# First modulation quarter loaded in halves ahead of the weights, its row ahead of the broadcast, and products on zeros on TensorE

## The chip, the cores and the metric

The kernel runs on one core of a Trainium2 chip. The metric is the device time of one execution in microseconds; lower is better. Before the change it is 1782.46 us, the median of three runs (1781.53 to 1785.64). The profile comes from one more execution, which took 1778.15 us.

## The reference

The computation is one inference step of a small hybrid model: 128 context tokens and 512 latent tokens of width 1024 pass through two layers. The first layer is a Mamba-2 mixer, the second is differential attention; each is followed by a gated convolutional channel mixer. The change touches only what comes first: the conditioned norm ahead of the Mamba-2 mixer, and the first products with its input weights.

```python
def modulation(cvec, w, b):
    m = jax.nn.silu(cvec) @ w + b
    return jnp.split(m[:, None, :], 6, axis=-1)

def modulate(x, g, shift, scale):
    return rmsnorm(x, g) * (1 + scale) + shift
# layer 0
hp = modulate(xp, norm_mix_g[i], p_sh1, p_sc1)   # context tokens, conditioned by c_ctx
hs = modulate(xs, norm_mix_g[i], s_sh1, s_sc1)   # latent tokens, conditioned by c
proj = h @ in_w                                  # inside ssd_mixer
```

So before the first product with `in_w`, three things must exist: the root mean square of every token, the shift and scale of each channel (a product of SiLU(c) with 1024 x 2048 numbers of the modulation weights), and the scaled tokens.

## The kernel before

The tokens stand transposed: eight tiles `x0` to `x7` of 128 channels by 640 tokens (512 latent, 128 context). The function `first_tiles` holds everything that the change touches. It runs under a hand-written order: each engine executes its instructions in the order in which the code emits them, and waits only where data is missing. Nearly every instruction goes through helpers, so the profile gives one line (L95) for all of them; the tile names tell them apart.

- **Loads.** One queue, SP's, issues all loads of this stage in order: the condition `c`, the constants `cst`, the eight `x` tiles, two weight tiles `raw` (first the narrow one for dt, then the first full one), two small tables (`modb`, `gains`), the first quarter of the modulation weights (`mp`, eight transfers of 256 KB), a third weight tile, and the three other quarters. One transfer waits for the eighth before it.
- **The silu of the condition** (`s`) is made ahead of all this, by ScalarE and two VectorE instructions, from `c`.
- **Statistics.** ScalarE and VectorE square the `x` tiles in turn (`sq`); TensorE sums them with a matrix of ones into `ms`. VectorE makes the reciprocal root from it in nine small instructions (`rs_v`, `rs_a`, `rs_y`), and TensorE spreads the result over 128 partitions (`nbc`).
- **Modulation.** `rows(q, k0, k1)` multiplies `s` with a quarter of the modulation weights into four row strips (`modrow`). ScalarE copies them (`modrow_s`); `finish(q)` transposes them on TensorE (`modt`), adds the bias (`mod`) and makes the gain (`gs`) on VectorE. A quarter q holds shift and scale for the tiles 2q and 2q+1.
- **Operands.** `cast(u)` splits a weight tile into a rounded part `whi` (ScalarE) and the rest `wlo` (VectorE). `scaled(i)` multiplies `x` with the spread root (`h`, VectorE). `high(i)` makes the rounded, modulated operand `h00h` on ScalarE and the same number unrounded on VectorE (`h`, a TENSOR_SCALAR); `low(i)` subtracts them into `h00l`.
- **Products.** `dense(tiles, k)` adds, for channel tile k and each weight tile, three products into PSUM: `h00h` with `whi` (operation 0), `h00h` with `wlo` (1) and `h00l` with `whi` (2). The `rows` of the next quarter stand between them.

After this stage the Mamba-2 mixer runs under a scheduler that sets the order on each engine from its own reckoning; from the channel mixer on, the order is the same in both kernels.

Of the kernel before, what the change touches and what calls it, by code (L numbers as in the profile page):

```python
# [355 lines left out]
class Step:  # L356
# [220 lines left out]

    def rms_bcast(self, alloc, sq, t0, t1, count, wait=4, behind=False):


        n = (t1 - t0) // 4
        y = self.rms_rows(sq, t0, n, count, behind)
# [6 lines left out]
    def rms_rows(self, sq, t0, n, count, behind=False):  # L589

        ms = self.bank("m", "ms")
        gate = self.last if behind else None
        for i, s in enumerate(sq):
            for j in range(4):
                o = self.mm(ms[32 * j:32 * j + 32, :n], self.ones, s[:, t0 + j * n:t0 + (j + 1) * n],
                            i == 0, i == len(sq) - 1)
                if behind:
                    self.hold(o, [gate])
        y = self.pc.tile([P, 160], F32, tag="rs_y", name="rs_y", bufs=1)[:, :n]
        with self.urgent(1.6) if self.later else nullcontext():  # L600
            self.rsqrt(y, ms[:, :n], n, count)
        return y
# [221 lines left out]
    def first_tiles(self, h, pool):  # L824
# [12 lines left out]

        def rows(q, k0, k1):

            if k0 == 0:  # L840
                self.rowps = self.bank("y", "modrow")
            for k in range(k0, k1):
                for j in range(4):
                    self.mm(self.rowps[32 * j:32 * j + 32, :P], self.s32[:, k, :], parts[q][:, k, j * P:(j + 1) * P],
                            k == 0, k == KT - 1)
            if k1 == KT:
                self.row = self.slot("f", "modrow_s", bufs=NF)
                self.act(self.row[:, :P], self.rowps[:, :P], AF.Copy)

        def finish(q):  # L850
            pt = self.bank("m", "modt")
            nc.tensor.transpose(pt[:, :P], self.row[:, :P], self.ident)
            i0 = 2 * q
            mv = self.mod[0][:, 0:16, :].rearrange("p (s i) c -> p s i c", s=2)[:, :, i0:i0 + 2, :]
            bv = self.modb[:, 0:16].rearrange("p (s i) -> p s i", s=2)[:, :, i0:i0 + 2]
            self.tt(mv, pt[:, :P].rearrange("p (s i r) -> p s i r", s=2, i=2)[:, :, :, 0:2],
                    bv.unsqueeze(3).to_broadcast([P, 2, 2, 2]), ALU.add)
            self.stt(gs[:, i0:i0 + 2, :], self.mod[0][:, 8 + i0:10 + i0, :], 1.0,
                     self.gains[:, i0:i0 + 2].unsqueeze(2).to_broadcast([P, 2, 2]), ALU.add, ALU.mult)

# [5 lines left out]
        def high(i):  # L866
# [5 lines left out]
            for a0, b0, c in cond:  # L872
                nc.vector.tensor_scalar(f[:, a0:b0], t0[i][:, a0:b0], gs[:, i, c:c + 1], sh[:, i, c:c + 1], ALU.mult, ALU.add)

# [3 lines left out]

        def dense(tiles, k):

            for op in (0, 1, 2) if k < KT - 1 else (0, 2, 1):
                for ps, (hi, lo), m in tiles:
# [6 lines left out]
                    for p in "AB":  # L889
                        c0, c1 = HALF[p]  # L890
                        self.mm(ps[:n, PO + c0:PO + c1], wt, x[:, c0:c1], k + op == 0, k == KT - 1 and op == 1)

        self.cst = self.ct([P, 3 * P + 36], "cst")
        nc.sync.dma_start(self.cst, a["cst"])
        for i in range(KT):
            xi = self.xslot(f"x{i}")
            nc.sync.dma_start(xi, a["xT"][i])
            self.x.append(xi)
        self.prefetch(1)
        self.load_consts()  # L900
        gs, sh = self.gs[0][0], self.shift(0, 0)
        load(0)
        self.prefetch(2)
# [4 lines left out]
        for i in range(KT):  # L908
            if i % 2:
                self.tt(sq[i], self.x[i], self.x[i], ALU.mult)  # L910
            else:
                self.act(sq[i], self.x[i], AF.Square)
        st = self.rms_bcast(lambda: self.wide("nbc"), sq, 0, T, D)
        next(st)
        self.cast(0)
        self.cast(1)
        rows(0, 0, 3)
        try:
            next(st)
# [24 lines left out]
        for q in range(1, 4):  # L944
            k = 2 * q
            if q == 1:
                dense(ws[2:], 0)
                finish(q)
                dense(ws[2:], 1)
            else:  # L950
                dense(ws[:1], k - 1)
                finish(q)
                dense(ws[1:], k - 1)
# [1054 lines left out]
def _layout(i):  # L2008
# [8 lines left out]
    m = n["mod_w"][0]  # L2017
    d["modp"] = m[:, :2048].reshape(KT, P, 2, 4, 256).transpose(3, 1, 0, 2, 4).reshape(4, P, KT, 512)
    d["mod0"] = m[:, 2048:].reshape(KT, P, 4 * D)
# [58 lines left out]
```

## Time and profile before

| what | value |
|---|---|
| median of three runs | 1782.46 us (1781.53 to 1785.64) |
| the profiled execution | 1778.15 us, span 1776.4 us |
| mean granted TensorE clock | 0.997 |
| TensorE busy | 1741.9 us, 98% of the span |
| VectorE busy | 1471.9 us, 83% |
| ScalarE busy | 1169.3 us, 66% |
| first product with `in_w` | starts at 22.70 us |
| read from memory | 248.32 MB, 159 GB/s over the span |

The span runs from the first instruction to the last; the execution's own time is 1.75 us longer. A row of a timeline gives start, duration, engine, the operation with what it writes and reads, a count, and in brackets the idle time before it with what ended it. A row with a count above 1 lasts from the start of the first to the end of the last. [...]

### The profile page before, as it was taken

What the parts mean: (1) busy time and instruction counts of PE and PEld (TensorE: products, weight loads), DVE (VectorE), ACT (ScalarE), POOL (GpSimd) and SP (SyncE); (2) the same over time, 40 slices, a digit from 0 to 9 for tenths busy, and PEclk for the clock granted to TensorE, in tenths of its full rate; (3) what the DMA queues carried; (4) which work ended last, traced back from release to release, by engine and by line L of the source; (5) the groups of instructions that cost most, each with busy time, mean ns of one, the idle gap of its engine ahead of it and who ended that gap; (6) DMA issues with size and microseconds to landing.
All of it is one profiled execution on the core that took longest, in us unless ns stands there. A gap on an engine that the chain in (4) does not pass through costs nothing.

```text
span 1776.4 us, 33599 instructions
## 1 busy us (share of the span) xinstructions
PE 1741.9 (98%) x12786; PEld 1665.6 (94%) x12786; DVE 1471.9 (83%) x2947; ACT 1169.3 (66%) x2313; POOL 150.2 (8%) x180
## 2 busy tenths in 40 slices
PE   7999999999999999999999999999999999999997
PEld 5899898989989999999999999999889999999997
DVE  6689999999966879798689799899778677967686
ACT  3479696979624767666675578877547566756661
POOL 0000000000000111211210000000001012121210
PEclk9999999999999999999999999999999999999998
DMA  9844244445663686978877365666137458786882
GB/s 346 271 143 139 101 123 147 111 141 167 221 216 135 143 208 151 252 180 218 190 167 245 117 170 135 158 156 164 56 121 205 117 144 199 176 194 158 171 234 80
DMA packets 120206, 300.66 MB, mean 169 GB/s; under 512 B 13950, under 2 KB 21738, under 8 KB 120044
## 3 DMA queue, kind: packets, MB, share of 16 engines
q1 hardware_dynamic: 94636, 231.79, 40.5%
q0 software_dynamic: 24832, 66.20, 21.1%
q8 instruction: 100, 1.64, 0.4%
q14 instruction: 62, 0.51, 0.1%
q10 hardware_dynamic: 576, 0.52, 0.1%
HBM read 248.32 MB, written 34.80 MB: 159 GB/s over the span
## 4 chain that ended last, share of the span: by engine, by line
PE 74%; DVE 4%; ACT 1%; issue 1%; DMA 0%; DVEq 0%; ACTq 0%
PE up L95 28%; PE po L95 24%; PE st L95 4%; PE v L348 2%; PE q L348 2%; PE k L348 2%; PE z L95 2%; PE sl L348 2%; PE ov L348 1%; PE po L348 1%; PE wt L348 1%; PE yp L95 1%; PE nbc L95 1%; PE modrow L95 0%; DMA ml<-cv 0%
## 5 line engine op out<-in xcount | busy, mean ns | idle before, releaser
L95 ACT ACTIVATE whi<-raw 128x1024 fp32r<-128x1024 f32 (+2 forms) x233 | 198.7, 855 | 162.9 <-PE po L95 76.6
L95 DVE TENSOR_TENSOR wlo<-raw,whi 128x1024 fp32r<-128x1024 f32 (+2 forms) x170 | 163.1, 966 | 54.2 <-ACT whi L95 53.7
L95 PE MATMUL po<-mh,whi 128*128 128x256 f32 (+1 forms) x704 | 165.4, 308 | 0.9 <-ACT y L95 0.7
L95 PE MATMUL po<-ml,whi 128*128 128x256 f32 (+1 forms) x704 | 164.6, 306 | 0.2 <-DMA ml<-cv 0.2
L95 PE MATMUL po<-mh,wlo 128*128 128x256 f32 (+1 forms) x704 | 164.4, 306 | 0.0
L95 DVE TENSOR_TENSOR wlo<-s,whi 128x512 fp32r<-128x512 f32 x136 | 91.5, 688 | 52.5 <-ACT whi L95 51.8
L95 POOL DMA_DIRECT2D wlo<-in_w_up x62 | 54.0, 871 | 942.7 <-ACT wlo L95 639.4
L95 PEld LDWEIGHTS po<-mh,whi 128*128 128x128 f32 x704 | 126.4, 188 | 2.0 <-ACT y L95 1.1
L95 PEld LDWEIGHTS po<-ml,whi 128*128 128x128 f32 x704 | 126.6, 188 | 0.4 <-DMA ml<-cv 0.4
L95 PEld LDWEIGHTS po<-mh,wlo 128*128 128x128 f32 x704 | 126.6, 188 | 0.0
L95 PE MATMUL up<-Th,wlo 128*128 128x320 f32 x408 | 125.9, 308 | 0.0
L95 PE MATMUL up<-Tl,whi 128*128 128x320 f32 x408 | 125.4, 307 | 0.0
L95 PE MATMUL up<-Th,whi 128*128 128x320 f32 x408 | 123.8, 303 | 0.2 <-ACT uraw L95 0.2
L95 PE MATMUL up<-h01h,wlo 128*128 128x320 f32 (+2 forms) x384 | 109.3, 308 | 0.0
L95 PE MATMUL up<-h11h,wlo 128*128 128x320 f32 (+2 forms) x384 | 109.1, 308 | 0.0
L95 PE MATMUL up<-h01l,whi 128*128 128x320 f32 (+2 forms) x384 | 108.8, 307 | 0.0
L95 PE MATMUL up<-h11l,whi 128*128 128x320 f32 (+2 forms) x384 | 108.8, 307 | 0.0
L95 PE MATMUL up<-h01h,whi 128*128 128x320 f32 (+2 forms) x384 | 107.8, 305 | 0.0
L95 PE MATMUL up<-h11h,whi 128*128 128x320 f32 (+2 forms) x384 | 107.7, 304 | 0.0
L95 ACT ACTIVATE whi<-s 128x512 fp32r<-128x512 f32 x136 | 83.3, 628 | 36.9 <-DVE s L95 33.1
L95 DVE SCALAR_TENSOR_TENSOR ca<-uraw,fcw,ca 128x511 f32<-128x511 f32 (+1 forms) x176 | 86.4, 548 | 11.2 <-ACT ca L95 9.6
L95 DVE SCALAR_TENSOR_TENSOR cv<-uraw,fcw,cv 128x511 f32<-128x511 f32 (+1 forms) x176 | 85.9, 548 | 4.9 <-ACT cv L95 4.8
(574 smaller groups left out, 5418.8 us busy)
## 6 DMA issues: line engine op xcount, KB each, us to landing
raw<-in_w_up SPq DMA_DIRECT2D x88, 512.0 KB
mw<-in_modT SPq DMA_DIRECT2D x44, 512.0 KB
raw<-in_w_in SPq DMA_DIRECT2D x40, 512.0 KB
rb<-rowd SPq DMA_DIRECT2D x40, 512.0 KB
wlo<-in_w_up POOLq DMA_DIRECT2D x36, 512.0 KB, 5.8
raw<-in_w_dn SPq DMA_DIRECT2D x64, 256.0 KB
raw<-in_w_qkv SPq DMA_DIRECT2D x24, 512.0 KB
mr<-in_mod SPq DMA_DIRECT2D x44, 256.0 KB
```

Of the source, the lines that this page charges most:

```text
L95: return later.record(self.name, method, call, args, kw) if later else call(*args, **kw)
L348: op.real = op.call(*(x.get() if isinstance(x, Lazy) else x for x in op.args), **op.kw)
```

## The change

The first quarter of the modulation weights is laid out anew in memory, so that its first 256 columns hold shift and scale of channel tile 0 and the others those of tile 1. It is loaded in two halves of four transfers each: the first half, behind `modb` and `gains`, stands ahead of the two weight tiles, the second behind them. `rows` and `finish` can do half a quarter; the first half's row, its transpose and its `mod` and `gs` now stand ahead of `nbc`. TensorE multiplies a block of bf16 zeros (`warm`, 128 x 512): 13 times ahead of the first sum of squares, twice between two sums, three times ahead of the first `modt` and three times behind it. For tiles 0 and 1 the unrounded operand moves from VectorE to ScalarE. The copy `bc` of the spread root moves behind both tiles, and operations 0 and 1 of a tile stand apart from operation 2.

```diff
@@ rms_rows
+            if between and i < len(sq) - 1:
+                between(2)
@@ first_tiles
+        def load_half(i):
+            if i == 0:
+                parts[0] = pool.tile([P, KT, 512], F32, tag="mp", name="mp0", bufs=4)
+            c = slice(256 * i, 256 * i + 256)
+            for k in range(0, KT, 2):
+                nc.sync.dma_start(parts[0][:, k:k + 2, c], a["modp"][0, :, k:k + 2, c])
...
+        def warm(n):
+            for _ in range(n):
+                self.mm(wps, zero[:, :P], zero[:, P:P + 512], True, True)
...
@@ high(i)
-                nc.vector.tensor_scalar(f[:, a0:b0], t0[i][:, a0:b0], gs[:, i, c:c + 1], sh[:, i, c:c + 1], ALU.mult, ALU.add)
+                if i < 2:
+                    self.act(f[:, a0:b0], t0[i][:, a0:b0], AF.Identity, scale=gs[:, i, c:c + 1], bias=sh[:, i, c:c + 1])
+                else:
+                    nc.vector.tensor_scalar(f[:, a0:b0], t0[i][:, a0:b0], gs[:, i, c:c + 1], sh[:, i, c:c + 1], ALU.mult, ALU.add)
...
+        zero = self.tmp("zero").bitcast(BF16)[:, :P + 512]
+        nc.vector.memset(zero, 0.0)
+        wps = self.dense_ps("warm")[:, :512]
+        warm(13)
...
-        self.prefetch(1)
         self.load_consts()
         gs, sh = self.gs[0][0], self.shift(0, 0)
-        load(0)
+        load_half(0)
+        self.prefetch(1)
+        load_half(1)
         self.prefetch(2)
...
-        st = self.rms_bcast(lambda: self.wide("nbc"), sq, 0, T, D)
+        st = self.rms_bcast(lambda: self.wide("nbc"), sq, 0, T, D, between=warm)
         next(st)
+        rows(0, 0, KT, range(2))
+        warm(3)
+        finish(0, 1)
         self.cast(0)
-        self.cast(1)
-        rows(0, 0, 3)
+        warm(3)
         try:
             next(st)
         except StopIteration as e:
             bps = e.value
-        bc = self.slot("f", "bc", bufs=NF)
-        self.act(bc, bps, AF.Copy)
         scaled(0, bps)
-        scaled(1, bps)
+        self.cast(1)
         h.extend(self.new_h("h00"))
-        rows(0, 3, KT)
-        finish(0)
         ws = [(self.dense_ps("in"), self.wcast[i], P if i else 64) for i in range(2)]
         half = KT // 2
         high(0)
         low(0)
+        dense(ws, 0, (0, 1))
+        rows(0, 0, KT, range(2, 4))
+        scaled(1, bps)
+        dense(ws, 0, (2,))
+        finish(1, 1)
+        bc = self.slot("f", "bc", bufs=NF)
         high(1)
+        self.act(bc, bps, AF.Copy)
         low(1)
         self.cast(2)
         self.wi = 3
-        dense(ws, 0)
+        dense(ws, 1, (0, 1))
         rows(1, 0, half)
-        dense(ws, 1)
+        dense(ws, 1, (2,))
         rows(1, half, KT)
```

How the rows move is shown at three places. On VectorE, at the program's start, the kernel before has this order (`c` is the condition, `s` its silu):

```order
L95 SCALAR_TENSOR_TENSOR s_86<-s_86,c_84 128x256
L95 TENSOR_SCALAR s_86<-s_86 128x256
L95 TENSOR_TENSOR sq_163<-x_94 128x640
L95 TENSOR_TENSOR sq_165<-x_98 128x640
L95 TENSOR_TENSOR sq_167<-x_102 128x640
```

The changed kernel has:

```order
L95 SCALAR_TENSOR_TENSOR s_86<-s_86,c_84 128x256
L95 TENSOR_SCALAR s_86<-s_86 128x256
L95 MEMSET zero 128x320
L95 TENSOR_TENSOR sq_179<-x_110 128x640
L95 TENSOR_TENSOR sq_181<-x_114 128x640
```

The block of zeros is written behind the two instructions on the condition, and ahead of the first square.

On TensorE, from the spread root on, the kernel before has (the first weight tile is 64 columns wide for operation 2):

```order
L95 MATMUL nbc<-rs_y,cst 128x160 x4
L95 MATMUL modrow<-mp_122,s_86 32x128 x20
L95 MATMUL modt<-cst,modrow_s 128x128
L95 MATMUL in<-h00h_254,whi_223 128x256
L95 MATMUL in<-h00h_254,whi_223 128x384
L95 MATMUL in<-h00h_254,whi_226 128x256
L95 MATMUL in<-h00h_254,whi_226 128x384
L95 MATMUL in<-h00h_254,wlo_227 128x256
L95 MATMUL in<-h00h_254,wlo_227 128x384
L95 MATMUL in<-h00l_255,whi_223 64x256
```

The changed kernel has, from operation 1 of channel tile 0 on:

```order
L95 MATMUL in<-h00h_296,wlo_293 128x256
L95 MATMUL in<-h00h_296,wlo_293 128x384
L95 MATMUL modrow<-mp_134,s_86 32x128 x16
L95 MATMUL in<-h00l_297,whi_279 64x256
L95 MATMUL in<-h00l_297,whi_279 64x384
L95 MATMUL in<-h00l_297,whi_292 128x256
L95 MATMUL in<-h00l_297,whi_292 128x384
L95 MATMUL modt<-cst,modrow_s 128x64
L95 MATMUL in<-h00h_298,whi_279 128x256
```

The row and the transpose of channel tile 1 used to stand ahead of all products; now the row stands between operations 1 and 2 of tile 0, and the transpose behind operation 2.

On ScalarE, for the first two channel tiles, the kernel before has:

```order
L95 ACTIVATE whi_226<-raw_110 128x1024
L95 ACTIVATE bc<-nbc 128x640
L95 ACTIVATE modrow_s<-modrow 128x128
L95 ACTIVATE h00h_254<-h_250,mod_116,gs_118 128x512
L95 ACTIVATE h00h_254<-h_250,mod_116,gs_118 128x128
L95 ACTIVATE h00h_256<-h_252,mod_116,gs_118 128x512
L95 ACTIVATE h00h_256<-h_252,mod_116,gs_118 128x128
L95 ACTIVATE whi_310<-raw_131 128x1024
```

The changed kernel has:

```order
L95 ACTIVATE h00h_296<-h_290,mod_128,gs_130 128x512
L95 ACTIVATE h00h_296<-h_290,mod_128,gs_130 128x128
L95 ACTIVATE h_316<-h_290,mod_128,gs_130 128x512
L95 ACTIVATE h_316<-h_290,mod_128,gs_130 128x128
L95 ACTIVATE modrow_s<-modrow 64x128
L95 ACTIVATE h00h_298<-h_345,mod_128,gs_130 128x512
L95 ACTIVATE h00h_298<-h_345,mod_128,gs_130 128x128
L95 ACTIVATE h_358<-h_345,mod_128,gs_130 128x512
L95 ACTIVATE h_358<-h_345,mod_128,gs_130 128x128
L95 ACTIVATE bc<-nbc 128x640
L95 ACTIVATE whi_363<-raw_147 128x1024
```

Two more instructions per channel tile stand on ScalarE, and the second tile's row copy, the copy `bc` and the third weight tile's rounding come behind them.

More of the change, by code (lines that the diff above doesn't have):

```diff
@@ L576, in rsqrt, with rms_bcast @@
         self.root = self.stt(y, a, 5.0, y, ALU.add, ALU.mult)
-    def rms_bcast(self, alloc, sq, t0, t1, count, wait=4, behind=False):
+    def rms_bcast(self, alloc, sq, t0, t1, count, wait=4, behind=False, between=None):
         n = (t1 - t0) // 4
-        y = self.rms_rows(sq, t0, n, count, behind)
+        y = self.rms_rows(sq, t0, n, count, behind, between)
         yield wait
@@ L587, in rms_bcast, with rms_rows @@
         return bc
-    def rms_rows(self, sq, t0, n, count, behind=False):
+    def rms_rows(self, sq, t0, n, count, behind=False, between=None):
         ms = self.bank("m", "ms")
@@ L836, in load, with rows @@
                 nc.sync.dma_start(parts[q][:, k, :], a["modp"][q, :, k, :])
-        def rows(q, k0, k1):
+        def load_half(i):
[4 more added lines that the diff above has]
+                nc.sync.dma_start(parts[0][:, k:k + 2, c], a["modp"][0, :, k:k + 2, c])
+        def rows(q, k0, k1, js=range(4)):
             if k0 == 0:
@@ L842, in rows, with finish @@
             for k in range(k0, k1):
-                for j in range(4):
-                    self.mm(self.rowps[32 * j:32 * j + 32, :P], self.s32[:, k, :], parts[q][:, k, j * P:(j + 1) * P],
+                for j in js:
+                    r = 32 * (j - js[0])
+                    self.mm(self.rowps[r:r + 32, :P], self.s32[:, k, :], parts[q][:, k, j * P:(j + 1) * P],
                             k == 0, k == KT - 1)
             if k1 == KT:
+                n = 32 * len(js)
                 self.row = self.slot("f", "modrow_s", bufs=NF)
-                self.act(self.row[:, :P], self.rowps[:, :P], AF.Copy)
-        def finish(q):
+                self.act(self.row[:n, :P], self.rowps[:n, :P], AF.Copy)
+        def finish(i0, n=2):
             pt = self.bank("m", "modt")
[L852 to L859, printed above, removed]
+            r = 64 * n
+            nc.tensor.transpose(pt[:, :r], self.row[:r, :P], self.ident[:r, :r])
+            mv = self.mod[0][:, 0:16, :].rearrange("p (s i) c -> p i s c", s=2)[:, i0:i0 + n]
+            bv = self.modb[:, 0:16].rearrange("p (s i) -> p i s", s=2)[:, i0:i0 + n]
+            self.tt(mv, pt[:, :r].rearrange("p (i s r) -> p i s r", s=2, i=n)[:, :, :, 0:2],
+                    bv.unsqueeze(3).to_broadcast([P, n, 2, 2]), ALU.add)
+            self.stt(gs[:, i0:i0 + n, :], self.mod[0][:, 8 + i0:8 + i0 + n, :], 1.0,
+                     self.gains[:, i0:i0 + n].unsqueeze(2).to_broadcast([P, n, 2]), ALU.add, ALU.mult)
+        def warm(n):
+            for _ in range(n):
+                self.mm(wps, zero[:, :P], zero[:, P:P + 512], True, True)
         def scaled(i, r):
@@ L877, in low, with dense @@
             self.tt(h[i][1], full.pop(i), h[i][0].bitcast(F32), ALU.subtract)
-        def dense(tiles, k):
-            for op in (0, 1, 2) if k < KT - 1 else (0, 2, 1):
+        def dense(tiles, k, ops=(0, 1, 2)):
+            for op in ops if k < KT - 1 else (0, 2, 1):
                 for ps, (hi, lo), m in tiles:
@@ L947, in first_tiles @@
                 dense(ws[2:], 0)
-                finish(q)
+                finish(k)
                 dense(ws[2:], 1)
@@ L951, in first_tiles @@
                 dense(ws[:1], k - 1)
-                finish(q)
+                finish(k)
                 dense(ws[1:], k - 1)
@@ L2017, in _layout @@
     m = n["mod_w"][0]
-    d["modp"] = m[:, :2048].reshape(KT, P, 2, 4, 256).transpose(3, 1, 0, 2, 4).reshape(4, P, KT, 512)
+    d["modp"] = m[:, :2048].reshape(KT, P, 2, 4, 2, P).transpose(3, 1, 0, 4, 2, 5).reshape(4, P, KT, 512)
     d["mod0"] = m[:, 2048:].reshape(KT, P, 4 * D)
```

## The prediction

> **What bounds the kernel now.** I read the busy time by stages first (length; then busy time and count of PE, weight loads, DVE, ACT, POOL; PE clock; DMA share; GB/s):
>
> ```profile
> 0.00:22.70 22.70, 11.55 (x137) 5.27 (x138) 11.20 (x23) 8.18 (x12) 0.20 (x4) 1.00 0.94 333
> 22.70:50.00 27.30, 27.24 (x324) 23.71 (x325) 19.44 (x38) 12.16 (x23) 0.00 (x0) 1.00 1.01 360
> 50.00:350.00 300.00, 297.82 (x2321) 271.33 (x2322) 275.41 (x557) 228.96 (x530) 0.00 (x0) 1.00 0.46 142
> ```
>
> From 22.70 us on TensorE hardly idles, so what moves the start of that dense work moves the end. Before it, TensorE is busy half the time. The most that any change of the start can give is part of those 22.7 us. The timeline of TensorE there:
>
> ```profile
> 7.60 1.48 PE L95 MATMUL ms<-sq,cst 128*32 128x160 f32 x16 [0.66 <-DVE sq L95]
> 13.07 0.76 PE L95 MATMUL ms<-sq,cst 128*32 128x160 f32 x8 [0.16 <-DVE sq L95]
> 15.16 2.00 PE L95 MATMUL modrow<-mp,s 128*32 128x128 f32 x24 [1.33 <-DMA mp<-in_modp]
> 17.09 2.11 PE L95 MATMUL nbc<-rs_y,cst 128*128 128x160 f32 x8
> 19.13 1.30 PE L95 MATMUL modrow<-mp,s 128*32 128x128 f32 x40
> 22.70 1.13 PE L95 MATMUL in<-h00h,whi 128*128 128x256 f32 x4 [1.55 <-ACT h00h L95]
> 23.95 0.79 PE L95 MATMUL in<-h00l,whi 128*64 128x256 f32 x4
> 24.67 1.08 PE L95 MATMUL modrow<-mp,s 128*32 128x128 f32 x32
> 25.68 0.85 PE L95 MATMUL in<-h00h,whi 128*128 128x256 f32 x4
> 26.65 0.74 PE L95 MATMUL in<-h00l,whi 128*64 128x256 f32 x4
> 27.32 1.08 PE L95 MATMUL modrow<-mp,s 128*32 128x128 f32 x32
> 28.33 0.57 PE L95 MATMUL in<-h00h,whi 128*128 128x256 f32 x2
> 29.32 0.27 PE L95 MATMUL modt<-cst,modrow_s 128*128 128x128 f32 x1
> 31.40 1.13 PE L95 MATMUL in<-h00h,whi 128*128 128x256 f32 x6
> ```
>
> Between 22.70 and 31.40 there is no bracket: TensorE waits for nothing. VectorE's timeline gives the chain ahead of that:
>
> ```profile
> 3.79 0.29 DVE L95 TENSOR_SCALAR s<-s 128x256 f32<-128x256 f32 x1
> 13.90 0.33 DVE L95 TENSOR_SCALAR rs_v<-ms 128x160 f32<-128x160 f32 x1 [0.88 <-PE ms L95]
> 16.70 0.33 DVE L95 SCALAR_TENSOR_TENSOR rs_y<-rs_a,rs_y 128x160 f32<-128x160 f32 x1
> 17.54 1.22 DVE L95 TENSOR_TENSOR wlo<-raw,whi 128x1024 fp32r<-128x1024 f32 x1
> 19.97 1.55 DVE L95 TENSOR_TENSOR h<-x,nbc 128x640 f32<-128x640 f32 x2 [1.21 <-ACT bc L95]
> 21.44 0.16 DVE L95 TENSOR_TENSOR mod<-modt,modb 128x8 f32<-128x8 f32 x1
> 23.07 0.83 DVE L95 TENSOR_TENSOR h00l<-h,h00h 128x640 fp32r<-128x640 f32 x1 [0.43 <-ACT h00h L95]
> 29.63 0.17 DVE L95 TENSOR_TENSOR mod<-modt,modb 128x8 f32<-128x8 f32 x1 [1.49 <-PE modt L95]
> ```
>
> and ScalarE's:
>
> ```profile
> 14.29 1.06 ACT L95 ACTIVATE whi<-raw 128x1024 fp32r<-128x1024 f32 x1 [0.79 <-DMA raw<-in_w_in]
> 19.23 0.70 ACT L95 ACTIVATE bc<-nbc 128x640 f32<-128x640 f32 x1 [3.89 <-PE nbc L95]
> 21.83 2.29 ACT L95 ACTIVATE h00h<-h,mod,gs 128x512 fp32r<-128x512 f32 x4 [1.06 <-DVE gs L95]
> 30.03 2.29 ACT L95 ACTIVATE h00h<-h,mod,gs 128x512 fp32r<-128x512 f32 x4 [1.22 <-DVE gs L95]
> ```
>
> So two chains meet at 21.83: the statistics (`ms`, root, `nbc`, `bc`, `h`) and the modulation row. Both are slow at their start, because TensorE runs slowly there. Equal shapes early and late (min/median/max ns), a later `nbc` of eight records, and dense pairs of 640 columns:
>
> ```profile
> L95 PE MATMUL ms<-sq,cst 128*32 128x160 f32 x64 | 6.0, 474 | 7.8 <-ACT sq L95 6.2 <-DVE sq L95 1.7
> L95 PE MATMUL ms<-gsq,cst x32: 299/312/324, 192.1 to 475.2; 128*32 128x160 f32 x32
> 544.02 1.10 PE L95 MATMUL nbc<-rs_y,cst 128*128 128x64 f32 x8
> 52.87 0.46 PE L95 MATMUL x<-h00h,whi 128*128 128x256 f32 x2
> 53.16 0.46 PE L95 MATMUL x<-h00l,whi 128*128 128x256 f32 x2
> ```
>
> 474 ns against 312 ns, 2.11 us against 1.10 us: the array is about half as fast until somewhere inside `nbc`, and fast from 19.13 on (40 records in 1.30 us). The PE clock column says 1.00 all the time and does not show this.
>
> **The products on zeros.** They do not start in the first microsecond: the zeros are written behind the `s` instruction that ends at 3.79 + 0.29 = 4.08 us. Writing them costs between a near-nothing and that same 0.29 us, which is nearest in shape; so the first product runs at about 4.45 us. A fast product costs 512 columns at 0.29 us per 640 columns (53.16 - 52.87) = 0.24 us, a slow one about 2.11/1.10 = 1.9 times that, 0.46 us. When does the array get fast? Before, it did so some 3.5 us after it became nearly unbroken at 15.16. Then 4.45 + 3.5 = 8.0; 7.6 products slow, 5.4 fast (1.3 us), and the first `ms` starts at 9.3 instead of shortly ahead of 7.60. From there one `ms` takes about 0.30 us (half of 1.48/2 less its tail) and two products 0.48 us: seven intervals of 0.78 us, 5.45 us, put the last `ms` at 14.75 instead of 13.07. It ends after 0.76 x 312/474 = 0.50 us, at 15.25 instead of 13.83. The statistics are late by d = +1.4 us. Bounds: if the products cost no time, the last `ms` still waits for its square at 13.07 and ends at 13.57, d = -0.3. If it takes twice the 3.5 us, to 11.4, all 13 are slow (10.4), the first `ms` and two products too (12.0), then six intervals: 16.7 + 0.5, d = +3.4. Changing between weight shapes may cost something: operation 2 of tile 0 takes 24.67 - 23.95 = 0.72 up to the next shape, where two pairs take 0.58. At that 0.14 once in each of six intervals d is 4.2 at most; the 32 records of 24.67 to 25.68 (1.01 us, against 32 x 1.30/40 = 1.04) show no such cost, and I take none.
>
> [...]
>
> **Statistics to first operand.** The root ends at 17.03 + d. `nbc` costs between 1.10 and 2.11 us; fast, by the ratio of equal shapes, 2.11 x 312/474 = 1.4 us. `h` no longer waits for `bc`, the wait in its bracket: it starts at 17.03 + 0.06 + 1.4 = 18.5 + d, takes 0.8, and `h00h` of tile 0 starts at 19.3 + d instead of 21.83. The half row is there by then. Loads stay the same up to `x7`; half 0 (1.05 MB at the 386 GB/s of the row below, 2.7 us) pushes the full weight tile from 14.29 to 17.0, and its ScalarE rounding (1.06) ends at 18.1, under cover. Its `wlo` (1.22) follows `h` and ends at 20.5 + d, just when operation 1 wants it. Half 1 lands where the whole quarter did, by 20.0 (no idle in the 40 records from 19.13). Its runs of 1 KB in place of 2 KB have no row; between no cost and twice the time of the half (2.7 us) I take none, with 2 us of cover.
>
> ```profile
> 15.00:17.00 2.00, 1.81 (x24) 0.60 (x24) 1.83 (x7) 0.35 (x1) 0.00 (x0) 1.00 1.05 386
> ```
>
> **First operand to second.** This is where the gain goes. From the start of `h00h` to the first product is 22.70 - 21.83 = 0.87 us, so TensorE starts at 20.2 + d. But the second channel tile no longer has its gain ready. It waits for: four ScalarE instructions (2.29) because the unrounded operand has left VectorE, `h00l` (0.04 + 0.83), operation 2 of tile 0, behind which the transpose is queued on TensorE (0.05 + 24.67 - 23.95 = 0.77), transpose to `mod` (29.63 - 29.32 = 0.31), `mod` and `gs` to ScalarE (30.03 - 29.63 = 0.40). Sum 4.64 us from one `h00h` to the next: 23.9 + d, products of tile 1 at 24.8 + d. Before, 25.68 - 22.70 = 2.98 us lay between the two. Operations 0 and 1 take 23.95 - 22.70 = 1.25, the half row 25.68 - 24.67 = 1.01; operation 2 needs `h00l` at 23.9 + 2.29 + 0.87 = 27.1 + d, takes 0.05 + 27.32 - 26.65 = 0.72, then the second half row 1.01. The dense work arrives at what was 28.33 at 28.85 + d: **+0.5 + d**.
>
> **The third tile.** ScalarE has, behind the second tile, `bc` 0.70 and the rounding 1.06 (28.0 + d); VectorE then has `wlo` 1.22 and two `h` 1.55 ahead of `mod` and `gs` 0.40: `h00h` of tile 2 at 31.15 + d, its product 0.87 later, at 32.0. TensorE itself comes there at 28.85 + 31.40 - 28.33 = 31.9 + d. That adds 0.1; the slack that was 0.5 (30.03 + 0.87 against 31.40) is used up.
>
> **After it.** The Mamba-2 stage's scheduler sets other orders. TensorE idles there 300 - 297.82 = 2.2 us in all; it could lose all of that, or as much again could appear; no row says which way, so 0 with bounds of 2.2 each way. Loads have room: they only become needed later.
>
> **Sum.** 0.5 + 1.4 + 0.1 = +2.0 us. Against the profiled execution: 1778.15 + 2.0 = 1780.15. The median stands 4.3 us above that execution; the same 2.0 on it gives **1784.5 us**. With d from -0.3 to 3.4 the forecast's own range is +0.3 to +4.0, 1782.8 to 1786.5.
>
> **Rivals.**
>
> *Faster: the chain between the operands is hidden.* Were ScalarE and VectorE ahead of TensorE all along, it would start at 20.2 - 0.3 and do 28.33 - 22.70 = 5.63 us plus half a row and a transpose (0.5 + 0.3). That ends at 26.3. But the next quarter (2.1 MB) and a weight tile (0.5 MB) land 2.6/0.386 = 6.8 us behind half 1, at 26.8, and its row ends at 27.1: -1.2 us, 1781.3. For it: TensorE waits for nothing there now. Against it: the queue order, with the transpose behind operation 2.
>
> *Slower: the 13 products hold the queue while the array is slow.* TensorE works its queue in order, so every sum of squares stands behind them. Should it get fast only near 11.4, d is 3.4 to 4.2, the change +4.0 to +4.8: 1786.9 in the middle. It exceeds 0.2% from d = 3.0 on. For it: seven products slow already fill 3.5 us. Against: the one start in the trace took 3.5 us, not 7. [...]
>
> *The products do not do what they are for: zeros leave the array slow.* Then 13 slow products, and seven intervals of 0.74 + 0.92 = 1.66 us: the last `ms` at 10.4 + 11.6 = 22.0, ending at 22.8, d = 9; with a slow `nbc` +10, 1792.5. For it: no row shows products on zeros. Against it: the array got fast after any unbroken work so far. [...]
>
> **How the numbers follow.** Forecast 0.60, faster rival 0.17, slow-products rival 0.17, zeros rival 0.03, something else 0.03. About 0.2%, 3.6 us, is what a measurement of this kernel can tell. Of the forecast, 0.07 of chance lies beyond +3.6 by d and the scheduler's 2.2; of the slow-products rival 0.11, and the zeros rival all: slower 0.21. Faster by 3.6 needs the faster rival and the scheduler's whole gain, 0.07 with what I have not seen. The rest, 0.72, is no change. The range reaches from the faster rival with half the scheduler's gain, 1780.2, to the slow rival with half its loss, 1788.0.
>
> **What would show it.** First product on zeros at 4.4 to 4.6 us; first `ms` at 9 to 10; last `ms` ending at 15.2 (13.6 to 17.2); `nbc` 1.4 us long; no `bc` wait ahead of `h`; first dense product at 21.6 and the second tile's 4.6 us behind it, with waits of TensorE for `h00l` and for the second `h00h`; the row that started at 28.33 before starting near 30.3. I am wrong if the last `ms` ends by 13.8, if the second tile follows within 3.5 us, or if TensorE's idle time between 50 and 350 us moves by more than 2 us.

## The result: slower by 0.55%, and the profile after

The changed kernel takes 1793.62 us (median of six executions, 1791.23 to 1796.38), the kernel before, beside it, 1784.06 us (six, 1781.53 to 1787.76). The ratio is 1.0055, with a 95% interval of 1.0043 to 1.0067: slower by 9.6 us, where I had forecast +2.0 and let the range end at 1788.0. The profiled execution took 1796.03 us, its span 1794.0.

TensorE's timeline of the changed kernel, up to the row that started at 28.33 us before:

```profile
4.48 5.65 PE L95 MATMUL warm<-zero 128*128 128x512 bf16 x13 [4.48 <-DVE zero L95]
10.06 0.48 PE L95 MATMUL ms<-sq,cst 128*32 128x160 f32 x8
10.47 0.60 PE L95 MATMUL warm<-zero 128*128 128x512 bf16 x2
11.01 0.48 PE L95 MATMUL ms<-sq,cst 128*32 128x160 f32 x8
...
16.69 0.48 PE L95 MATMUL ms<-sq,cst 128*32 128x160 f32 x8
16.98 1.92 PE L95 MATMUL modrow<-mp,s 128*32 128x128 f32 x32
...
20.45 1.31 PE L95 MATMUL nbc<-rs_y,cst 128*128 128x160 f32 x8
23.52 1.12 PE L95 MATMUL in<-h00h,whi 128*128 128x256 f32 x4 [1.76 <-ACT h00h L95]
24.86 1.94 PE L95 MATMUL modrow<-mp,s 128*32 128x128 f32 x32
26.73 0.80 PE L95 MATMUL in<-h00l,whi 128*64 128x256 f32 x4
...
29.02 1.12 PE L95 MATMUL in<-h00h,whi 128*128 128x256 f32 x4 [1.29 <-ACT h00h L95]
...
34.63 0.56 PE L95 MATMUL in<-h00h,whi 128*128 128x256 f32 x2
```

Four things can be read here. The thirteen products take 0.43 us each ((10.06 - 4.48)/13) and the two between sums 0.27 us each ((11.01 - 10.47)/2): the array was slow through all thirteen. From one sum to the next it is 0.95 us (11.01 - 10.06), so the last sum ends at 17.17 instead of 13.83. A half row, 16 products that leave 32 records, takes 1.92 us; 32 records of a whole row took 1.08 before. And at 34.63 the dense work stands 6.30 us behind the kernel before.

The clock column, in the windows of TensorE, shows one more loss (window; length, then busy time of PE, PEld, DVE, ACT, POOL; PE clock; DMA share; GB/s):

```profile
26.99:30.40 3.41, 2.12 (x15) 1.40 (x14) 0.32 (x2) 2.37 (x6) 0.00 (x0) 1.00 1.05 387
30.40:33.81 3.41, 3.41 (x45) 2.58 (x48) 2.62 (x3) 1.58 (x3) 0.00 (x0) 0.50 1.05 387
```

For one window of 3.41 us the granted clock is 0.50, right behind a window in which TensorE was 62% busy (2.12 of 3.41). That costs 1.5 us: from the second tile's first product to the last row above it is 5.61 us (34.63 - 29.02), and 4.09 us in the second execution shown below, where the clock holds (32.22 - 28.13).

VectorE's timeline and ScalarE's, for the chain between:

```profile
17.23 0.32 DVE L95 TENSOR_SCALAR rs_v<-ms 128x160 f32<-128x160 f32 x1 [4.31 <-PE ms L95]
21.80 0.82 DVE L95 TENSOR_TENSOR h<-x,nbc 128x640 f32<-128x640 f32 x1 [0.57 <-PE nbc L95]
24.98 0.82 DVE L95 TENSOR_TENSOR h00l<-h,h00h 128x640 fp32r<-128x640 f32 x1 [1.23 <-ACT h L95]
27.76 0.16 DVE L95 TENSOR_TENSOR mod<-modt,modb 128x4 f32<-128x4 f32 x1 [1.23 <-PE modt L95]
```

```profile
22.66 1.20 ACT L95 ACTIVATE h00h<-h,mod,gs 128x512 fp32r<-128x512 f32 x2 [1.97 <-DVE h L95]
28.16 1.20 ACT L95 ACTIVATE h00h<-h,mod,gs 128x512 fp32r<-128x512 f32 x2 [1.04 <-DVE gs L95]
```

On these two engines the chain has the shape that I had drawn: `rs_v` waits for the sums (4.31 us), `h` for `nbc` and no longer for `bc`, `h00l` for ScalarE's unrounded `h`, `mod` for the transpose, and the second `h00h` for the gain. On TensorE one wait is missing: operation 2 does not wait for `h00l`, which is there at 25.80 (24.98 + 0.82). It starts at 26.73, without idle time, when the half row ahead of it is done.

**Behind this stage** I follow the lag of a row, its start less that of the same row in the first profile of before. In the Mamba-2 mixer's output stage, before and after:

```profile
427.22 1.13 PE L95 MATMUL st<-xw,bt 128*128 128x512 f32 x2
```

```profile
437.32 1.13 PE L95 MATMUL st<-xw,bt 128*128 128x512 f32 x2
```

The lag is 10.1 us there; 3.8 more were lost in the mixer. TensorE waits twice for `xt` there in the changed kernel:

```profile
103.88 1.10 PE L95 MATMUL xtp<-cst,xf 128*128 128x128 f32 x8 [1.36 <-ACT xt L95]
...
396.03 0.66 PE L95 MATMUL xtp<-cst,xf 128*128 128x128 f32 x4 [0.66 <-ACT xt L95]
```

All waits for `xt` between 45 and 420 us come to 2.0 us after, 0.6 before. At the end the lag is 17.6 us (the spans), although from the channel mixer on the order of every engine is the same: another 7.5 us that no instruction of the change explains. So before any reason is tested, the spread of one profile has to be known.

### The profile page after: what moved, and what is told of

The parts are those of the page before. It is cut to its first block, busy times and chain, and to the rows that moved or that the text cites. A ratio compares the mean times of both kernels' runs of the same rounds, so it can differ in the third digit from the quotient of the medians.

```text
span 1794.0 us, 33673 instructions
## 1 busy us (share of the span) xinstructions
PE 1759.2 (98%) x12820; PEld 1676.9 (93%) x12820; DVE 1471.6 (82%) x2946; ACT 1172.2 (65%) x2318; POOL 150.2 (8%) x180
## 4 chain that ended last, share of the span: by engine, by line
PE 72%; DVE 4%; ACT 2%; DMA 1%; issue 1%; DVEq 0%; ACTq 0%
PE up L95 28%; PE po L95 24%; PE st L95 4%; PE q L348 2%; PE k L348 2%; PE v L348 2%; PE sl L348 2%; PE ov L348 1%; PE po L348 1%; PE z L95 1%; PE wt L348 1%; PE yp L95 1%; PE nbc L95 0%; DMA q<-q 0%; PE modrow L95 0%
## 5 line engine op out<-in xcount | busy, mean ns | idle before, releaser
L95 DVE SCALAR_TENSOR_TENSOR ca<-uraw,fcw,ca 128x511 f32<-128x511 f32 (+1 forms) x176 | 86.1, 544 | 11.4 <-ACT ca L95 9.7
```

The source lines that it names most:

```text
L95: return later.record(self.name, method, call, args, kw) if later else call(*args, **kw)
```

## The experiments

Each kernel was timed beside the kernel before on the same chip; not all pairs ran on one chip, so medians are to be compared by their ratios. The lags in the table are against the first profile of before: at the row that started at 28.33 there, at the row that started at 427.22, and at the end of the span.

| kernel | lag at 28.33 | at 427.22 | at the end | median us | ratio, 95% interval |
|---|---|---|---|---|---|
| the change | 6.3 | 10.1 | 17.6 | 1793.62 | 1.0055 [1.0043, 1.0067] |
| the change, again | 3.9 | 5.4 | 14.4 | 1792.58, one | - |
| before, again | 2.8 | 1.8 | 6.8 | 1785.02, one | - |
| no products | 6.5 | 5.2 | 5.3 | 1783.59 | 1.0015 [1.0001, 1.0029] |
| products alone | 2.9 | 2.4 | 6.1 | 1784.64 | 1.0020 [1.0004, 1.0035] |
| zeros first | 5.0 | 3.3 | 10.8 | 1786.65 | 1.0021 [1.0007, 1.0035] |
| none between sums | 3.3 | 1.6 | 3.1 | 1783.02 | 1.0004 [0.9990, 1.0017] |
| gaps filled | 5.0 | 8.0 | 12.1 | 1789.80 | 1.0036 [1.0024, 1.0048] |
| half rows packed | 5.4 | 6.8 | 13.8 | 1793.20 | 1.0056 [1.0036, 1.0077] |
| early and held | 2.0 | 2.1 | 4.0 | 1784.14 | 1.0001 [0.9991, 1.0011] |
| change repaired | -0.1 | 0.2 | 6.8 | 1784.49 | 1.0000 [0.9990, 1.0010] |

**The spread first: both kernels once more.** Neither is edited.

> The changed kernel once more, for a second profile. If the mixer's loss is its order: the lag over the kernel before grows from the end of the first stage to 420 us by 3 to 5 us again, with the wait of TensorE for ScalarE's xt near 104 us and for xt and gsq near 394 us. If it was chance: it grows by less than 1.5. The clock's falls may stand elsewhere.

> The kernel before once more, for a second profile. The profiled execution was the fastest seen (1778 of 1778 to 1788). If the clock's falls make the spread: this one has a fall or two, in the first 40 us or near 1335 us, each with 1.7 us; if not, its time lies 3 us higher without one.

The changed kernel's second execution, on TensorE:

```profile
15.81 0.48 PE L95 MATMUL ms<-sq,cst 128*32 128x160 f32 x8
...
22.64 1.11 PE L95 MATMUL in<-h00h,whi 128*128 128x256 f32 x4 [1.76 <-ACT h00h L95]
...
28.13 1.13 PE L95 MATMUL in<-h00h,whi 128*128 128x256 f32 x4 [1.30 <-ACT h00h L95]
...
32.22 0.56 PE L95 MATMUL in<-h00h,whi 128*128 128x256 f32 x2
```

and the kernel before in its second one:

```profile
19.55 2.36 PE L95 MATMUL modrow<-mp,s 128*32 128x128 f32 x40
...
26.44 1.94 PE L95 MATMUL modrow<-mp,s 128*32 128x128 f32 x32
...
31.11 0.57 PE L95 MATMUL in<-h00h,whi 128*128 128x256 f32 x2
```

In the change the same instructions start 2.4 us earlier in the second execution (32.22 against 34.63): its array got fast earlier, so that the last sum ends at 16.29 and not 17.17, and its clock did not fall. In the kernel before they start 2.8 us later in the second (31.11 against 28.33): there the array was slow up to the 40 records (2.36 us, 1.30 in the first profile), and the clock fell over the row at 26.44. The profile on which I had argued was a lucky draw of the start; beside the first four experiments, before took 1778.12 to 1787.67 us over 31 executions. Compared by means of two draws each, the change costs 3.7 us at this row ((6.3 + 3.9)/2 - 2.8/2). In the mixer the change's lag grew by 1.5 us this time (3.9 to 5.4), between the 3 to 5 that I had named for its order and the less than 1.5 for chance: this run alone does not decide.

**No products.** The change without its products on zeros.

```diff
 def warm(n):
-    for _ in range(n):
-        self.mm(wps, zero[:, :P], zero[:, P:P + 512], True, True)
+    return
```

> The changed kernel without any product on zeros; all else of the change stays, and the mixer's order is the one of the kernel before. Theory P (the products cost most: they delay the last sum of squares by 3.3 us and change the mixer's order): the last sum ends at 13.8 as before, the row that starts at 28.33 before starts 2 to 4 us later (half rows on a slow array, the longer chain to the second operand), the mixer adds 0 to 1, the total is +2 to +4 over the kernel before. Theory R (the rearrangement of loads, rows and operands costs most): the 28.33 row is 5 us or more late, the total +6 to +10.

```profile
13.06 0.76 PE L95 MATMUL ms<-sq,cst 128*32 128x160 f32 x8 [0.30 <-DVE sq L95]
13.60 3.62 PE L95 MATMUL modrow<-mp,s 128*32 128x128 f32 x32
...
22.98 3.63 PE L95 MATMUL modrow<-mp,s 128*32 128x128 f32 x32
```

The sums end as before, d = 0, but each half row takes 3.6 us, because the array is slow in both (at the second by a fall of the clock that lasts two windows, from 20.51 us). So without products the rest of the change is 6.5 us late in this execution, as theory R had it. Yet the time is only 0.15% above before, 2.7 us, which is theory P's, and the lag shrinks from 6.5 to 5.2 by 427 us: the mixer's order is here the one of the kernel before. Neither theory holds whole. The scheduler reckons with the products too: without them the change's loads, rows and operands leave its order as it was.

**Products alone.** The kernel before, with the zeros, thirteen products and two between sums.

```diff
...
+        zero = self.tmp("zero").bitcast(BF16)[:, :P + 512]
+        nc.vector.memset(zero, 0.0)
+        wps = self.dense_ps("warm")[:, :512]
+        warm(13)
...
-        st = self.rms_bcast(lambda: self.wide("nbc"), sq, 0, T, D)
+        st = self.rms_bcast(lambda: self.wide("nbc"), sq, 0, T, D, between=warm)
```

> The kernel before with the products on zeros alone (13 ahead of the sums, two between each pair of them); loads, rows and operands as before. Theory P: the last sum ends at 17.2 instead of 13.8, the 28.33 row comes 2.5 to 3.5 us late, the mixer, which has about the changed kernel's order, adds 3 to 4, total +5.5 to +7.5. Theory R: total 0 to +2, since the row and the weights, not the sums, set the start.

```profile
4.38 4.60 PE L95 MATMUL warm<-zero 128*128 128x512 bf16 x13 [4.38 <-DVE zero L95]
9.85 0.48 PE L95 MATMUL ms<-sq,cst 128*32 128x160 f32 x8
...
15.53 0.48 PE L95 MATMUL ms<-sq,cst 128*32 128x160 f32 x8
...
19.25 1.35 PE L95 MATMUL nbc<-rs_y,cst 128*128 128x160 f32 x8 [2.48 <-DVE rs_y L95]
```

The products do make the array fast: `nbc` takes 1.35 us, against 2.11 and 2.50 in the two profiles of before. Here the thirteen take 4.60 us and not 5.65, so only some eight are slow, and the last sum still ends 2.2 us late (16.01 against 13.83). What remains when the array is fast early is the interval between sums, 0.95 us ((15.53 - 9.85)/6). TensorE then waits 2.48 us for the root, and the kernel is 0.20% slower. That is 3.5 us, less than the 5.5 to 7.5 expected, because the mixer adds nothing: the lag goes from 2.9 to 2.4. Its order here is one of its own, the nearest to the change's; on TensorE it differs from that in four places, all before 110 us.

**Zeros first.** The change, with the block of zeros written ahead of the two silu instructions on VectorE.

```diff
+        self.zero = self.tmp("zero").bitcast(BF16)[:, :P + 512]
+        self.nc.vector.memset(self.zero, 0.0)
...
-        zero = self.tmp("zero").bitcast(BF16)[:, :P + 512]
-        nc.vector.memset(zero, 0.0)
+        zero = self.zero
```

> The changed kernel with the zeros written ahead of the silu of the condition, so that the 13 products can start near 0.5 us. If the late products are the loss at the start: products from 0.5 to 6.1, the array fast by 4 to 7.5, the last sum ends at 13.5 to 14.2, the first dense product starts at 20 to 20.8, the 28.33 row is 1 to 2.5 us late without a clock drop and up to 4 with one; the mixer has a third order, its part is open (-1 to +4). If the products are innocent: the 28.33 row is 6 us late as in the changed kernel.

```profile
13.16 0.48 PE L95 MATMUL ms<-sq,cst 128*32 128x160 f32 x8
...
21.93 3.37 PE L95 MATMUL modrow<-mp,s 128*32 128x128 f32 x32
```

With the products started some three microseconds earlier, the sums are not late at all (13.64 against 13.83). But two falls of the clock, at 22.25 and 29.08, lie on the second tile, and a half row takes 3.37 us. The row came 5.0 us late, where I had expected 4 at most with a fall: part of what was won at the sums was lost again to the clock. The ratio falls from 1.0055 to 1.0021; the mixer's order is yet another one, whose lag shrinks by 1.7 us up to 427 us, so the gain is not the start's alone.

**None between sums.** The change with its thirteen products, and none between the sums.

```diff
-        st = self.rms_bcast(lambda: self.wide("nbc"), sq, 0, T, D, between=warm)
+        st = self.rms_bcast(lambda: self.wide("nbc"), sq, 0, T, D)
```

> The changed kernel with the 13 products at the start, but none between the sums of squares. If the products between are half of the delay: the first sum still starts at 10.1, the last one ends at 13.5 to 14, the first dense product starts at 20 to 21, the 28.33 row is 1 to 2.5 us late without a clock drop. If only the 13 count: the last sum ends near 16 and the row is 4 us late or more. The array may fall back to slow where TensorE now idles between sums; then the half row takes over 3 us.

```profile
12.96 0.48 PE L95 MATMUL ms<-sq,cst 128*32 128x160 f32 x8 [0.55 <-DVE sq L95]
```

The last sum waits for its square again and ends at 13.44: the fourteen products between the sums are what held the statistics. This one edit brings the ratio back to 1.0004. By the profiles, the sums end 2.9 to 3.7 us earlier. Only 0.6 to 3.0 us of that reach the row of 28.33, since the clock falls at 21.03 and the second half row takes 2.90 us. Some 4 us more lie in the mixer: from 28.33 to 427.22 the lag falls by 1.7 us here, under the same order as in the kernel above, where it rose by 3.8 and 1.5 in the change. So the edit acts twice, and only the first of the two is the products' work on TensorE; no run parts the two.

**Gaps filled.** The change, with seven products on zeros behind `nbc` and five behind the second tile's transpose, where TensorE waits 1.76 and 1.29 us. The order on VectorE, ScalarE and SP is that of the change, row for row.

```diff
...
+        warm(7)
         scaled(0, bps)
...
         finish(1, 1)
+        warm(5, self.bank("y", "warm2"))
```

> The changed kernel with seven more products on zeros between the spread root and the first dense product and five more between the second tile's transpose and its products, that is, in TensorE's two idle gaps; VectorE, ScalarE and SP keep the changed kernel's order in every row. If idle gaps make the clock fall: no fall at 20 to 34 us, and the 28.33 row comes 4.4 to 4.8 us late instead of 6.3; the mixer still adds 3 to 4.5 up to 420 us, total +7 to +9. If the clock falls for another reason: it falls again and the row stays 6 us late or more.

```profile
23.69 1.13 PE L95 MATMUL in<-h00h,whi 128*128 128x256 f32 x4 [0.25 <-ACT h00h L95]
...
29.19 1.13 PE L95 MATMUL in<-h00h,whi 128*128 128x256 f32 x4
...
33.29 0.57 PE L95 MATMUL in<-h00h,whi 128*128 128x256 f32 x2
```

The clock did not fall here: from 29.19 to the row at 33.29 it is 4.10 us, against 5.61 in the change and 4.09 in its second execution. From one operand to the next it is 5.50 us still, as in both profiles of the change: the interval belongs to the chain, not to the clock. The row is 5.0 us late (4.4 to 4.8 expected), the mixer adds 3.0, and the time is 0.36% above before, 6.4 us (7 to 9 expected). The ratio of 1.0036 lies below the change's interval, and the two intervals overlap. Since the change's second execution had no fall there without any filling, this one profile does not show that the filling is the reason; it shows what a start without the fall is worth.

**Half rows packed.** The change, with even and odd k of a half row on separate strips, so that four strips work, and one more addition on VectorE.

```diff
+                g = 4 // len(js)
                 for j in js:
-                    r = 32 * (j - js[0])
+                    r = 32 * (j - js[0] + len(js) * (k % g))
...
```

> The changed kernel with each half row spread over all four row strips (even and odd k apart, added on VectorE behind the transpose). If a half row on two strips costs as much as a whole one: each falls from 1.9 to about 1.0 us on a fast array, the second tile follows the first after 4.6 to 4.9 us instead of 5.5, and the 28.33 row comes about 0.9 us earlier (5.4 late with a clock fall, 3.7 without). If the half row is hidden: no change there. The mixer's order is another one, its part is open.

```profile
16.09 1.06 PE L95 MATMUL modrow<-mp,s 128*32 128x128 f32 x32
...
24.69 1.94 PE L95 MATMUL modrow<-mp,s 128*32 128x128 f32 x32
```

The first half row takes 1.06 us instead of 1.92: the same 32 records on four strips. On four strips the records start four at a time, a group every 0.11 us (24.67, 24.80, 24.91 in the kernel before); on two they start in pairs, and a pair takes 0.11 us as well (16.98, 17.09, 17.20 in the change's first profile). So a half row on two strips costs nearly as much as twice the records on four. The second was slow again, 1.94 us, because the clock stood at 0.50 for two windows from 21.78 on, behind one that was 48% busy. From the first operand to the second it is 6.97 us (29.59 - 22.62) for that, and not the 4.6 to 4.9 expected. The time does not move (1.0056): the half row saved waits for the root (TensorE idles 0.85 us ahead of `nbc`), and the fall takes the rest.

**Early and held.** The kernel before, with the zeros first, thirteen products, one between sums, four ahead of the rows and six ahead of the first dense product; VectorE's block of zeros aside, all other engines have the order of before.

```diff
...
+                between(1)
...
+        warm(4)
         rows(0, 0, 3)
...
         finish(0)
+        warm(6)
```

> The kernel before (its loads, rows, operands and its mixer order in every row of ScalarE and SP) with products on zeros that cost no time: zeros written first, 13 products, one between two sums, four ahead of the first rows and six ahead of the first dense product. If products pay once they are early, short and fill the idle gaps: the array fast by 4 to 8 us and no fall up to 50 us, the last sum ends at 13.5, the spread root takes 1.3 us, the 28.33 row comes at 27.5 to 28.3, the mixer adds 0 to -1.2, total -1 to -3 against the kernel before, which starts slow or falls once in some executions. If products on TensorE are a loss in themselves: +1 or more.

```profile
19.18 0.42 PE L95 MATMUL modrow<-mp,s 128*32 128x128 f32 x8 [0.71 <-DMA mp<-in_modp]
...
21.21 0.43 PE L95 MATMUL modrow<-mp,s 128*32 128x128 f32 x8 [0.24 <-DMA mp<-in_modp]
...
22.20 2.52 PE L95 MATMUL warm<-zero 128*128 128x512 bf16 x6
```

With a fast array the row no longer sets the pace: the transfers of the quarter do, up to 21.21. Behind a window that was 62% busy the clock falls at 22.44, so the six products took 0.42 us each, and the first dense product starts at 24.16. The row of 28.33 came at 30.37, where 27.5 to 28.3 was expected. The ratio is 1.0001, so the gain of 1 to 3 us is not seen; the interval reaches from 1.6 us faster to 2.0 slower. In this execution the first quarter landed no sooner than in the first profile of before (there its rows were through by 20.43, 19.13 + 1.30), and the clock fell; so the ratio does not tell what a fast array that stays fast would give.

**Change repaired.** The change with the costs found above taken out, and with three moves that no other run has (the transpose, the next half row, the unrounded operand): zeros first, one product between sums, packed half rows, the second tile's transpose ahead of operation 2, the next half row ahead of the second tile's products, the second tile's unrounded operand back on VectorE, and seven products behind `nbc`. The scheduler then gives the mixer the order of the kernel before.

```diff
...
-                between(2)
+                between(1)
...
-                if i < 2:
+                if i < 1:
...
+        warm(7)
...
-        dense(ws, 0, (2,))
         finish(1, 1)
+        dense(ws, 0, (2,))
+        rows(1, 0, half)
...
-        dense(ws, 1, (0, 1))
-        rows(1, 0, half)
-        dense(ws, 1, (2,))
+        dense(ws, 1)
...
```

> The changed kernel with its costs taken away one by one: zeros written first, one product between sums, half rows on four strips, the second tile's transpose ahead of operation 2, the next row's first half ahead of tile 1's products, the unrounded operand of tile 1 back on VectorE, seven products ahead of the first dense product. Its mixer order on ScalarE is that of the kernel before. If late sums, half rows, the chain between the operands, clock falls and the mixer's order are the whole loss: first dense product at 20.5, the second tile's at 24.8 to 25.4, the 28.33 row at 27.6 to 28.8, no clock fall, the mixer 0 to -1.2, total -3 to 0. If something else of the change costs time: +2 or more.

```profile
20.26 1.13 PE L95 MATMUL in<-h00h,whi 128*128 128x256 f32 x4 [0.25 <-ACT h00h L95]
...
25.15 0.42 PE L95 MATMUL modrow<-mp,s 128*32 128x128 f32 x8 [0.24 <-DMA mp<-in_modp]
25.50 0.85 PE L95 MATMUL in<-h00h,whi 128*128 128x256 f32 x4
...
28.21 0.56 PE L95 MATMUL in<-h00h,whi 128*128 128x256 f32 x2
```

The first dense product starts 2.4 us earlier than before, the second tile 5.24 us behind it, now held by the landing of the next quarter (25.15) and just later than the 24.8 to 25.4 expected, and the row of 28.33 at 28.21. The ratio is 1.0000. So the costs named, taken out together, remove the whole loss. What is won is at most the 1.5 us by which this row stands ahead of the mean of the two profiles of before, and the interval of 0.1% each way can't show that much. Seven edits at once do not tell the share of each; for that stand the runs above.

## Why the prediction was wrong

The forecast sum was 0.5 + 1.4 (d) + 0.1. Three things in it failed: d came out at 2.5 to 3.3, the half row inside the 0.5 was 0.9 us too short, and the mixer, put at nothing, added 1.5 to 3.8. A fourth, a fall of the clock, was in no term. Two executions of the change against the steps (times in us):

| step | forecast | first profile | second |
|---|---|---|---|
| first product on zeros | 4.45 | 4.48 | 4.55 |
| first sum starts | 9.3 | 10.06 | 9.18 |
| from sum to sum | 0.78 | 0.95 | 0.95 |
| last sum ends (d) | 15.25 (+1.4) | 17.17 (+3.3) | 16.29 (+2.5) |
| first dense product | 21.6 | 23.52 | 22.64 |
| first operand to second | 4.64 | 5.50 | 5.49 |
| row of 28.33 starts | 30.3 | 34.63 | 32.22 |
| lag gained in the mixer | 0, bounds 2.2 | 3.8 | 1.5 |

**The products on zeros: the mechanism held, d was too small.** Their start, their price when slow (0.43 against 0.46) and the first sum were right in the second execution. What failed is the interval, "one `ms` takes about 0.30 us" and "two products 0.48 us": it is 0.41 (10.47 - 10.06) and 0.54, so 0.95 and not 0.78, seven times. That is 1.2 us. I had seen such a cost at a change of shape (0.14), kept it in the bounds and taken none. The rest of d is the rise of the array, 3.5 us after the first product in the second execution, 5.4 in the first, in which all thirteen were slow. So the rival of the 13 products that hold the queue met its d of 3.4 in one of the two starts, but not by its own account alone: the array was fast at 9.9 and not near 11.4, and 1.2 us came from the intervals. The 3.5 us that I took was one draw, from the first profile of before; the other runs have rises of 2.9 us ("none between sums"), 3.3 ("products alone") and 5.7 ("gaps filled") behind the first product. One reading of mine was wrong without harm: 2.11 against 1.10 us for `nbc` compares 160 columns with 64, not equal shapes.

**Statistics to first operand: right.** The first dense product at 20.2 + d gives 23.5 and 22.7. `nbc` took 1.31 us (forecast 1.4), `h` no longer waited for `bc`, and weights and loads stayed under cover.

**First operand to second: the term of the half row was mis-sized.** I took 1.01 us for a half row, by a row with as many records. It takes 1.92 on two strips, where records start in pairs and not in fours, and operation 2 with the transpose behind it is 0.86 us later for that. "Half rows packed" showed it: 1.06 us on four strips. With it the path changed. In my sum operation 2 waited for `h00l`, and the half row was done at the same moment (20.2 + 1.25 + 1.01 against 19.3 + 2.29 + 0.87, both 22.46 + d). In both profiles the half row came last and the wait of TensorE for `h00l`, which I had named as a sign, did not appear. The waits behind it, for the transpose and for the gain, were as named.

**What no step had: the clock that falls.** I had taken the array to stay fast once it was. In the first profile the fall cost 1.5 us. With the measured sizes the forecast of the start closes: 0.5 + 3.3 (d) + 0.9 (half row) + 1.5 (clock) = 6.2 against 6.3, and 0.5 + 2.5 + 0.9 = 3.9 against 3.9 in the second. (The 0.1 for the third tile did not appear: its first product comes 3.07 us behind this row in both kernels, 37.70 - 34.63 and 31.40 - 28.33.) But the kernel before pays such a fall as well (a late rise and a fall, together 2.8 us, in its second execution), so only a part of this is the change's.

**After it: the sign was open, and it came out at the far end.** Under the scheduler's new order the lag grew in the mixer by 3.8, 1.5 and 3.0 us in the three profiles with that order (the change twice, gaps filled), and by -1.0, -1.2, 0.0 and 0.3 in the four others with the order of before (before again, no products, early and held, repaired). I had bounded this term by TensorE's idle time, and that left out a part: between the two rows TensorE idles 4.5 us in the mean of the three and 3.1 in the mean of those with the order of before (its first profile included), but it is also busy for longer with the same products, 397.2 us against 395.4. So some 1.4 us are idle time and some 1.8 longer busy time, for which no run gives a reason. The waits for `xt` are no proof: early and held waits 1.7 us for it and lost nothing. That the order is the cause rests on these groups; no kernel had this order behind the start of the kernel before, and with the order nearest to it, in products alone, the lag fell by 0.5 us.

**The sum.** 3.7 us at the start, by the means of two draws, and some 3 us by the mixer's order make about 7 of the 9.6 measured. The rest falls behind 427 us, where the instructions and their order are the same: lags there grew by 7.5, 9.0 and 4.1 us in the three profiles with the change's order, by 5.0, 0.1, 1.9 and 6.6 in the four with that of before. Much of it can be told apart in the rows. Of the 7.5 us in the change's first profile, 1.3 come with the fall of the clock near 1344 us and 3.5 in a slow stretch behind it (both in the last section); of the 9.0 in its second, 2.0 around a fall at 813.62 and 3.5 in the same stretch. The repaired kernel and the second profile of before have that stretch too, and the first profile of before, against which all lags are taken, has neither the stretch nor a fall ahead of 1766.29, in its last 10.1 us. Whether the remaining 2 to 3 us are more than this spread stays open.

**The chances.** I counted the slow-products rival and the mixer's bounds as separate mishaps, each small. Several terms erred to the same side, and I gave +9.6 us no room.

## What to carry to other kernels

A filler on an engine that works its queue in order was free here only where the next work was not yet there: what stands between two sums was paid once for each sum here (0.95 us a round, with the change of shape), although the engine had been idle there before. A split of a small product into halves should keep all four strips busy, or it costs nearly what the whole one costs (here 1.92 us on two strips and 1.06 on four, with 2 x 1.08 for a whole row). And one profile is one draw: before a difference of a few microseconds is explained, the same kernel should be profiled a second time, and the order that a scheduler derives from the changed work should be compared as carefully as the edit itself.

## What the runs showed of the hardware

**Behind products on zeros the array got fast.** There is nothing in them but zeros, and the array was fast from 9.92 us on in the change, from 18.66 on in the first profile of before. In these profiles the granted clock changes on a grid of 3.41 us: in the change at 9.92, 30.40, 33.81, 1344.53 and 1347.94 us, and in the first profile of before at 18.66 and 1766.29, 512 steps apart. Where the products start at 4.4 to 4.6 us, the array was fast 2.9 to 5.7 us after the first of them, at the end of the first grid window in which TensorE was at least 85% busy. This is no threshold for other work: a window 87% busy in "no products" (10.27 to 13.69) and one 93% busy in the second profile of before (14.97 to 18.38) left the array slow, and it got fast one window later.

**The clock fell behind windows that were about half busy.** Every fall of the first 40 us came behind a grid window in which TensorE was 43% to 62% busy, with single waits of at most 1.8 us, and lasted one window, in two kernels two. No window there at or above 66% was followed by a new one; some between 48% and 62% were not either (20.16 to 23.57 in the change, 1.65 of 3.41 us busy, and 18.66 to 22.07 in the first profile of before, 2.10 of 3.41). The grid lies elsewhere in each execution (a border at 9.92 in the change, at 8.43 in the first profile of before, three steps ahead of 18.66), and that may decide, as a wait late in the program suggests, in the change and before:

```profile
1343.07 0.36 PE L95 MATMUL st<-h11h,whi 128*128 128x256 f32 x1 [1.84 <-ACT whi L95]
```

```profile
1330.28 0.36 PE L95 MATMUL st<-h11h,whi 128*128 128x256 f32 x1 [1.84 <-ACT whi L95]
```

The same wait of 1.84 us stands in both. In the change it lay inside one grid window (1.58 of 3.42 us busy), and the next had a clock of 0.51:

```profile
1341.05:1344.47 3.42, 1.58 (x14) 1.43 (x13) 3.42 (x8) 2.79 (x5) 0.00 (x0) 1.00 0.51 135
1344.47:1347.88 3.41, 3.41 (x43) 2.91 (x42) 2.36 (x6) 2.00 (x2) 0.10 (x1) 0.51 0.98 340
```

In the first profile of before the wait lay across a border of the grid, at 1329.38 (384 windows behind the rise at 18.66); the windows on its two sides were 72% and 74% busy (2.47 of 3.41 and 2.52 of 3.42 us), and no fall followed.

**The same work, 4.7% slower, at full clock.** For some 76 to 80 us from the rows of about 1355 us on (in the time of the first profile of before), six of the twelve profiles (both of the change and the second of before among them) work the same matmul rows more slowly: from row to row the lag grows by 4.7% of the time, about 3.5 us in all. Two windows over about the same rows, of before in its second execution and in its first, both without any idle time of TensorE:

```profile
1400.00:1440.00 40.00, 40.00 (x269) 40.00 (x269) 17.41 (x30) 21.77 (x44) 6.21 (x10) 1.00 0.54 158
```

```profile
1396.00:1436.00 40.00, 40.00 (x281) 40.00 (x280) 18.33 (x31) 22.07 (x45) 6.21 (x10) 1.00 0.58 173
```

269 instructions stand against 281 in 40 us, with a clock of 1.00 in both. The cause is open; no run was made for it.
